# Mixture-of-experts inside a two-block layer: the experts' TensorE instructions kept in written order, and SwiGLU with one vector instruction less

## The chip, the cores and the metric

The kernel runs on one core of a Trainium2 chip. The metric is the device time of one execution in microseconds (us); the time before is given as the median of three runs.

## The reference

Two transformer blocks follow each other on 256 tokens of 1024 features, all in float32. The first has an RWKV and an attention mixer, then a mixture of 32 experts; the second has a stick-breaking attention, an attention over 256 memory tokens and a dense layer of 4096 hidden units. The change lies in the experts. Every token goes to 4 of them, and each does this (cut):

```python
gu = xb @ w_gate_up[e] + b_gate_up[e]
gate = jnp.minimum(gu[:, :D_FF], SWIGLU_LIMIT)                  # 7.0
up = jnp.clip(gu[:, D_FF:], -SWIGLU_LIMIT, SWIGLU_LIMIT)
act = (up + 1.0) * gate * jax.nn.sigmoid(SWIGLU_ALPHA * gate)   # 1.702
return act @ w_down[e] + b_down[e]
```

## The kernel before, in words

The first block up to the routing takes the first 277 us or so, the experts the time up to about 1260 us, the second block the rest. Each of the 32 experts has 64 slots for tokens (a branch for experts with more follows the stage and is there whether it is taken or not).

**Weights.** An expert's weights come in six transfers of 2 MB each, four for the gate and up matrices and two for the down matrix, through one queue of SyncE (`stream`, line 110, called by `issue`, line 1021). They go into nine slots of SBUF, shared out by `slot`; a transfer is issued when the chunk that had its slot before is used up. Ahead of expert 21 one slot is given up for the memory tokens' keys and values and one is lent to their weights. The last expert's last transfer comes in four pieces of 512 KB. Behind it the same queue fetches the first two weight chunks of the second block.

**An expert on the engines.** `gate_up` (line 1104) has TensorE multiply the inputs `xe` of 64 tokens with the weights, k by k, into two PSUM banks, `pg` (gate) and `pu` (up), after the biases (`bgu`, three bfloat16 parts) went in by a matmul of their own. Then SwiGLU: four instructions of VectorE and one sigmoid of ScalarE make `u`. `down` (line 1127) transposes `u` on TensorE (`at`), ScalarE copies the result, and TensorE multiplies it with the down weights (`py`); VectorE puts the product, times the gate of the modulation, into `y`.

**Two at a time.** `gather` (line 1066) fetches the inputs of two experts by a matmul with a one-hot matrix that VectorE builds (`s`; `ga`), and transposes the weighted one-hot (`sw`; `swt`). `combine` (line 1149) adds what two experts made to their tokens, by a matmul (`cb`) that VectorE adds to x. In the program they stand between an expert's `gate_up` and its `down`: the gather after every odd expert, the sum after every even one but the first:

```python
act = gate_up(e, ws[:4])
if e % 2 and e + 1 < ne:
    gather(e + 1)
if e % 2 == 0 and e:
    combine(e - 2)
down(e, act, ws[4:])
```

**What sets the order.** Each engine runs its instructions in one fixed order. A scheduler with a timeline of its own sets that order when the program is built; it may move an instruction past others that it doesn't depend on. The order on TensorE is therefore not that of the program text.

**After the experts.** The second block transposes x (`x3t`, copied to `xh` and `xl`), and multiplies it with weights that ScalarE and VectorE or GpSimd split in a high and a low part first (`w3h` and `w3l`, lines 117 and 118; matmuls `d`, lines 1274 to 1276). The buffers of the split parts lie where the experts' buffers were.

Of the kernel before, what the change touches and what calls it, by code (L numbers as in the profile page):

```python
# [10 lines left out]
F32 = mybir.dt.float32  # L11
# [4 lines left out]
OP = mybir.AluOpType  # L16
# [7 lines left out]
# plain PSUM banks before the experts; buffers of the RWKV and of the stick-breaking attention; how many experts  # L24
# before the last one the memory tokens come in
NP, B4, NZ, ME = 4, 5, 5, 12

# columns of the packed per-feature vectors
# [14 lines left out]
# columns of the constants (they depend on shapes alone)  # L43
# [47 lines left out]

class Kernel:
# [11 lines left out]
    # ---- weights stream: one order, one queue, a ring of slots  # L104
# [8 lines left out]
    def split(self, pool, src, n, name, eng):  # L113
        """src = hi + lo exactly, each in float32r"""
        hi = pool.tile([128, n], F32R, tag=name + "h", name=name + "h")
        lo = pool.tile([128, n], F32R, tag=name + "l", name=name + "l")
        self.nc.scalar.activation(hi, src, AF.Copy)  # L117
        eng.tensor_tensor(lo, src, hi.bitcast(F32), op=OP.subtract)  # L118
        return hi, lo
# [21 lines left out]
    def setup(self):  # L141
# [9 lines left out]
        # what is not needed past the experts  # L151
        self.xe = ExitStack()
        cp = self.pool("cpe", es=self.xe)
        # x after the attention, its scale per token, and the norm's gain and shift with the modulation, per feature
# [28 lines left out]
    def rsqrt(self, out, src, eps=None, scale=1.0, refine=None):  # L183
        """(src * scale + eps) ** -0.5; with a pool to take temporaries from, one Newton step more"""
# [25 lines left out]
    # ================================================================ first block, before the experts  # L210
    def expert_bias(self, pool):
        """the gate and up biases as three exact bfloat16 parts, on 3 x 32 partitions"""
# [4 lines left out]
        nc.sync.dma_start(t[0:32], A["b_gate_up"])  # L217
        for i in range(3):
# [5 lines left out]
    def phase1(self):  # L224
# [9 lines left out]
        # ---- modulation rows: silu(c) @ w_ada + b_ada; the i-th 512 columns add up on the partitions i mod 32  # L234
# [7 lines left out]
        # two slots of the stream that are at first lent to the RWKV and the MoBA  # L242
# [24 lines left out]
        def gate_rows():  # L267
            """rows 4, 5, 10 and 11, for the gates: partition by partition, the bias on one of them"""
# [14 lines left out]
        def gate_bc(q):  # L283
            """a row of a gate on every partition"""
# [4 lines left out]
        def ada_col(r, i0):  # L289
            """rows i0..i0+3 as columns [feature, (row, 128 features)]"""  # L290
# [6 lines left out]
        # ---- x over its root mean square, transposed  # L297
# [29 lines left out]
        # ---- h = rms(x) * g1 * (1 + scale1) + shift1, transposed, as hi + lo  # L327
# [19 lines left out]
        # ---- projections  # L347
# [10 lines left out]
        def dense_T(src, ncols, tiles, consume):  # L358
            """features on partitions; tiles: (first column, columns) of the chunk; two to a bank"""
# [13 lines left out]
        def dense_N(src, consume, then=lambda: None):  # L373
            """tokens on partitions, 512 columns"""
# [21 lines left out]
        def shift_mix(dst, ps, m, mi):  # L396
            """p + (shift(p) - p) * mu"""
# [45 lines left out]
        # ---- RWKV, element by element: decays inside chunks of 64 steps, scaled keys and receptances  # L443
# [9 lines left out]
        for g in ((0, 2), (2, 4)):  # L453
# [3 lines left out]
            # k * k_k over its norm per head  # L457
# [10 lines left out]
            # k * (1 + (a - 1) * k_a)  # L468
# [18 lines left out]
        # ---- RWKV, chunk by chunk: two chunks of 64 steps side by side, eight heads  # L487
# [10 lines left out]
        def pairs(lhs, rhs, tt, name):  # L498
            """per head, [step of lhs, step of rhs]; even heads, then odd ones"""
# [8 lines left out]
        def sub(s):  # L508
            """superchunk s: everything that needs neither the inverse nor the state"""
# [11 lines left out]
            # (I - L)^T of every 16 steps, kept as [row, head, column of the block]  # L521
# [4 lines left out]
        def invert(s, r):  # L526
            """(I - L)^T of every 16 steps: column r times row r of L^T goes to the columns after r"""
# [22 lines left out]
        # ---- MoBA projections (one block, so plain causal attention with ALiBi)  # L550
# [1033 lines left out]
```

## Time and profile before

| what | us |
|---|---|
| median of three runs | 1592.47 |
| the three runs | 1592.47, 1597.8, 1590.65 |
| span of the profiled execution | 1590.6 |
| TensorE busy | 1449.3 (91%) |
| VectorE busy | 591.2 (37%) |
| ScalarE busy | 395.1 (25%) |
| transfers, mean over the span | 318 GB/s |

The profiled execution's own time is that of its span, 1590.6 us; it equals the fastest of the three runs. Busy shares are means over stages with different limits. A matmul in float32 has two records in the trace. A busy TensorE isn't one at its peak, and the granted clock has a line of its own. PE is TensorE, DVE VectorE, ACT ScalarE, POOL GpSimd, SP SyncE. A wait is put down to the instruction that came last.

### The profile page before, as it was taken

To read this page: it belongs to the slowest core of one execution; us is meant where nothing else is said; L and a number is where in the kernel's file an instruction comes from. 1 tells how busy PE (TensorE), PEld (TensorE's weight loads), DVE (VectorE), ACT (ScalarE), POOL (GpSimd) and SP (SyncE) were. 2 spreads that over 40 slices of the span, in tenths; PEclk is the share of its full clock that TensorE was granted. 3 is DMA by queue.
4 is the path that set the end of the run, shared out by engine and by line. 5 is a ranking of instruction groups with operands and counts; after the bars stand their busy time and mean duration, and the time that the engine had idled before them with its cause. 6 is when DMAs were issued, how large, how long until landed. Compare 5 with 4: busy or idle time off the path is not lost. (4 is left out here: it accounts for less than half of the span.)

```text
span 1590.6 us, 19145 instructions
## 1 busy us (share of the span) xinstructions
PE 1449.3 (91%) x7818; PEld 813.4 (51%) x7818; DVE 591.2 (37%) x1177; ACT 395.1 (25%) x767; POOL 212.6 (13%) x190
## 2 busy tenths in 40 slices
PE   5999998999999989988998989999989899899996
PEld 2976876333333323323333334433333497699995
DVE  2576877232122222221222122222221345555455
ACT  4862344110000000000001011110010366455553
POOL 1243751000000000000000000000000233252221
PEclk9999999999999999999999999999999999989998
DMA  9734747899999999999999997999999451535540
GB/s 337 251 120 170 280 170 288 340 417 416 418 416 416 418 418 415 419 418 415 418 418 415 397 409 319 411 416 416 418 417 414 154 208 54 195 123 180 191 159 27
DMA packets 115061, 505.15 MB, mean 318 GB/s; under 512 B 5548, under 2 KB 6572, under 8 KB 82168
## 3 DMA queue, kind: packets, MB, share of 16 engines
q1 hardware_dynamic: 114792, 503.74, 79.9%
q8 instruction: 63, 1.03, 0.3%
q14 instruction: 30, 0.25, 0.0%
q0 software_dynamic: 176, 0.14, 0.0%
HBM read 502.81 MB, written 1.05 MB: 317 GB/s over the span
## 5 line engine op out<-in xcount | busy, mean ns | idle before, releaser
L1139 PE MATMUL py<-w,at 128*64 128x512 f32 x1024 | 265.0, 669 | 22.0 <-ACT at L1134 21.8
L1117 PE MATMUL pg<-w,xe 128*64 128x512 f32 x1024 | 267.7, 598 | 0.0
L1117 PE MATMUL pu<-w,xe 128*64 128x512 f32 x1024 | 264.9, 592 | 0.0
L1121 ACT ACTIVATE sg<-g 128x512 f32<-128x512 f32 (+1 forms) x33 | 20.2, 616 | 601.6 <-DVE g L1120 601.6
L1139 PEld LDWEIGHTS py<-w,at 128*64 128x64 f32 x1024 | 77.4, 153 | 175.7 <-issue 141.6
L1146 DVE TENSOR_TENSOR y<-py,gate 64x512 f32<-64x512 f32 x64 | 44.1, 688 | 304.4 <-PE py L1139 303.7
L1117 PEld LDWEIGHTS pu<-w,xe 128*64 128x64 f32 x1024 | 74.1, 137 | 146.7 <-issue 146.6
L117 ACT ACTIVATE w3h<-w 128x512 fp32r<-128x512 f32 x184 | 115.2, 631 | 109.1 <-PE d L1275 57.6
L1117 PEld LDWEIGHTS pg<-w,xe 128*64 128x64 f32 x1024 | 70.9, 137 | 135.0 <-issue 130.2
L118 DVE TENSOR_TENSOR w3l<-w,w3h 128x512 fp32r<-128x512 f32 x132 | 94.2, 719 | 115.7 <-ACT w3h L117 111.0
L1120 DVE TENSOR_SCALAR g<-pg 128x512 f32<-128x512 f32 (+1 forms) x33 | 22.2, 675 | 295.4 <-PE pg L1117 295.4
L118 POOL TENSOR_TENSOR w3l<-w,w3h 128x512 fp32r<-128x512 f32 x52 | 67.4, 1301 | 432.1 <-ACT w3h L117 420.9
L1274 PE MATMUL d<-xh,w3h 128*128 128x256 f32 x352 | 100.5, 288 | 0.9 <-ACT xh L1261 0.9
L1210 POOL TENSOR_TENSOR wml<-w,wml 128x512 fp32r<-128x512 f32 x4 | 5.2, 1293 | 718.5 <-ACT wml L1209 718.5
L1275 PE MATMUL d<-xl,w3h 128*128 128x256 f32 x352 | 100.8, 287 | 0.1
L1276 PE MATMUL d<-xh,w3l 128*128 128x256 f32 x352 | 100.2, 286 | 0.0
L1133 PE MATMUL at<-ca,u 128*128 128x128 f32 x128 | 23.5, 313 | 63.8 <-DVE u L1124 63.8
L1083 PEld LDWEIGHTS ga<-s,xm 128*128 128x128 f32 x512 | 62.3, 197 | 28.2 <-issue 26.5
L1083 PE MATMUL ga<-s,xm 128*128 128x128 f32 x512 | 69.8, 288 | 1.2 <-DVE s L1073 1.2
L1274 PEld LDWEIGHTS d<-xh,w3h 128*128 128x128 f32 x352 | 68.4, 196 | 1.6 <-ACT xh L1261 1.3
L1275 PEld LDWEIGHTS d<-xl,w3h 128*128 128x128 f32 x352 | 68.4, 194 | 0.9 <-DVE xl L1263 0.6
L1276 PEld LDWEIGHTS d<-xh,w3l 128*128 128x128 f32 x352 | 68.2, 194 | 0.0
(421 smaller groups left out, 2100.6 us busy)
## 6 DMA issues: line engine op xcount, KB each, us to landing
w<-w_gate_up SPq DMA_DIRECT2D x128, 2048.0 KB, 16.7
w<-w_down SPq DMA_DIRECT2D x71, 2048.0 KB, 17.6
w<-w_ada SPq DMA_DIRECT2D x12, 2048.0 KB, 9.2
w<-w_up SPq DMA_DIRECT2D x8, 2048.0 KB, 7.5
w<-w_in SPq DMA_DIRECT2D x6, 2048.0 KB, 11.4
w<-w_in_sb SPq DMA_DIRECT2D x5, 2048.0 KB, 10.3
w<-w_out SPq DMA_DIRECT2D x4, 2048.0 KB, 7.7
w<-w_mem_kv SPq DMA_DIRECT2D x1, 2048.0 KB, 12.0
```

Source lines behind the costliest of these rows:

```text
L117: self.nc.scalar.activation(hi, src, AF.Copy)
L118: eng.tensor_tensor(lo, src, hi.bitcast(F32), op=OP.subtract)
L1083: PE.matmul(ps[:, k * 128:(k + 1) * 128], xm[:, a, (kk + k) * 128:(kk + k + 1) * 128], s[:, a], start=a == 0, stop=a == 1, skip_group_chec ...
L1117: PE.matmul(p[64 * h:64 * h + 64, :], xe[:, k], w[:, k % 2, c:c + 512], start=False, stop=k == 7)
L1120: DVE.tensor_scalar(g[:, c], pg[:, c], 7.0, None, op0=OP.min)
L1121: ACT.activation(s[:, c], g[:, c], AF.Sigmoid, scale=1.702)
L1133: PE.transpose(ps[:, j * 128:(j + 1) * 128], act[:, j * 128:(j + 1) * 128], ident)
L1139: PE.matmul(py[64 * h:64 * h + 64, :], at[:, j, c], ws[c][:, j, h * 512:(h + 1) * 512], start=c == 0 and j == 0, stop=c == 1 and j == 3)
L1146: DVE.tensor_tensor(st[e & ~1][2][r, hs], py[64 * h:64 * h + 64], self.gate2[64 * h:64 * h + 64, hs], op=OP.mult)
L1274: PE.matmul(o, wh[:, ws], xh[:, k], start=k == 0 and i % 2 == 0, stop=False, skip_group_check=True)
L1275: PE.matmul(o, wh[:, ws], xl[:, k], start=False, stop=False, skip_group_check=True)
L1276: PE.matmul(o, wl[:, ws], xh[:, k], start=False, stop=k == 7, skip_group_check=True)
```

## The change

1. The experts' matmuls and transposes go through a small class `InOrder`, which ties each to the one before it by a dependency without a semaphore, so that the scheduler leaves them in the order of the program text. The matmuls of the down bias (`bias_down`) and those of the memory tokens are issued as before, outside this chain.
2. SwiGLU: the sigmoid reads the gate's bank directly and is clamped afterwards at sigmoid(1.702 x 7) (`SIG_MAX`), the clamp of the gate goes into the multiplication, and the 1.0 that is added to `up` is added once to its bias (so its clamp runs from -6 to 8). VectorE has three instructions instead of four for each expert, and the tile `g` is gone.
3. For the last point one VectorE instruction is added where the biases are prepared.

The comments and docstrings of the program are dropped as well. The diff, cut:

```diff
+SIG_MAX = 1.0 / (1.0 + math.exp(-1.702 * 7.0))
...
+class InOrder:
+    def __init__(self, tc, last=None):
+        self.tc, self.last = tc, last
+
+    def _keep(self, i):
+        if self.last is not None:
+            self.tc.add_manual_dep(i.ins, self.last.name,
+                                   mybir.DependencyInfo(mybir.DependencyClass.NoSync, mybir.DependencyReason.DATA),
+                                   reason="in order")
+        self.last = i.ins
+        return i
+
+    def matmul(self, *a, **k):
+        return self._keep(self.tc.nc.tensor.matmul(*a, **k))
+
+    def transpose(self, *a, **k):
+        return self._keep(self.tc.nc.tensor.transpose(*a, **k))
...
     def expert_bias(self, pool):
...
         nc.sync.dma_start(t[0:32], A["b_gate_up"])
+        DVE.tensor_scalar(t[0:32, 1024:2048], t[0:32, 1024:2048], 1.0, None, op0=OP.add)
...
     def experts(self):
         nc, A = self.nc, self.A
-        PE, ACT, DVE, POOL = nc.tensor, nc.scalar, nc.vector, nc.gpsimd
+        PE, ACT, DVE, POOL = InOrder(self.tc), nc.scalar, nc.vector, nc.gpsimd
...
-            g, u, s = (pool.tile([128, 512], F32, tag=n, name=n, bufs=1) for n in ("g", "u", "sg"))
+            u, s = (pool.tile([128, 512], F32, tag=n, name=n, bufs=1) for n in ("u", "sg"))
             for c in cuts(e):
-                DVE.tensor_scalar(g[:, c], pg[:, c], 7.0, None, op0=OP.min)
-                ACT.activation(s[:, c], g[:, c], AF.Sigmoid, scale=1.702)
-                DVE.tensor_scalar(u[:, c], pu[:, c], 7.0, -7.0, op0=OP.min, op1=OP.max)
-                DVE.scalar_tensor_tensor(u[:, c], u[:, c], 1.0, g[:, c], op0=OP.add, op1=OP.mult)
-                DVE.tensor_tensor(u[:, c], u[:, c], s[:, c], op=OP.mult)
+                ACT.activation(s[:, c], pg[:, c], AF.Sigmoid, scale=1.702)
+                DVE.tensor_scalar(u[:, c], pu[:, c], 8.0, -6.0, op0=OP.min, op1=OP.max)
+                DVE.scalar_tensor_tensor(u[:, c], pg[:, c], 7.0, u[:, c], op0=OP.min, op1=OP.mult)
+                DVE.scalar_tensor_tensor(u[:, c], s[:, c], SIG_MAX, u[:, c], op0=OP.min, op1=OP.mult)
```

**Order on TensorE, an odd expert in the middle of the stage.** Before, in a row: the gather `ga` for the next pair, in pieces between the down projection of the expert before and the odd expert's own gate and up matmuls, and further on the end of these.

```order
L1083 MATMUL ga<-s,xm 128x128 x3
L1139 MATMUL py<-w,at 64x512 x8
L1083 MATMUL ga<-s,xm 128x128 x4
L1117 MATMUL pg<-w,xe 64x512 x2
L1117 MATMUL pu<-w,xe 64x512 x2
L1117 MATMUL pg<-w,xe 64x512 x2
L1117 MATMUL pu<-w,xe 64x512 x2
L1083 MATMUL ga<-s,xm 128x128 x7
```

```order
L1117 MATMUL pg<-w,xe 64x512 x2
L1117 MATMUL pu<-w,xe 64x512 x2
L1133 MATMUL at<-ca,u 128x128 x4
L1139 MATMUL py<-w,at 64x512 x8
L1110 LDWEIGHTS selb
```

With the change, the same place (L109 and L112 are the lines of the class `InOrder`):

```order
L109 MATMUL pg<-w,xe 64x512 x2
L109 MATMUL pu<-w,xe 64x512 x2
L109 MATMUL ga<-s,xm 128x128 x16
L112 MATMUL swt<-ca,sw 128x128 x2
L112 MATMUL at<-ca,u 128x128 x4
L109 MATMUL py<-w,at 64x512 x16
```

The gather and the transposes of `sw` now stand whole between the last gate and up matmuls and the transposes `at`, which followed these directly before.

**Order on TensorE, the even expert behind it**, with the change; before, the sum `cb` stood between the gate and up matmuls too:

```order
L109 MATMUL pg<-w,xe 64x512 x2
L109 MATMUL pu<-w,xe 64x512 x2
L109 MATMUL cb<-y,swt 128x512 x4
L112 MATMUL at<-ca,u 128x128 x4
L109 MATMUL py<-w,at 64x512 x16
L109 LDWEIGHTS selb
```

The sum has the gather's place here; the next expert's biases (`selb`) come after the whole down projection.

**Order on VectorE, an odd expert**, before:

```order
L1120 TENSOR_SCALAR g<-pg 128x512
L1122 TENSOR_SCALAR u<-pu 128x512
L1123 SCALAR_TENSOR_TENSOR u<-u,g 128x512
L1089 TENSOR_SCALAR xe<-ga,sc_71,sh_72 128x128 x2
L1124 TENSOR_TENSOR u<-u,sg 128x512
L1089 TENSOR_SCALAR xe<-ga,sc_71,sh_72 128x128 x2
L1146 TENSOR_TENSOR y<-py,gate_74 64x512 x2
```

and with the change:

```order
L1146 TENSOR_SCALAR u<-pu 128x512
L1147 SCALAR_TENSOR_TENSOR u<-pg,u 128x512
L1148 SCALAR_TENSOR_TENSOR u<-sg,u 128x512
L1114 TENSOR_SCALAR xe<-ga,sc_71,sh_72 128x128 x2
L1098 TENSOR_SCALAR s<-ca,Rm,rs 128x64 x4
L1098 TENSOR_SCALAR sw<-ca,Rm,W 128x64 x4
L1114 TENSOR_SCALAR xe<-ga,sc_71,sh_72 128x128 x2
L1170 TENSOR_TENSOR y<-py,gate_74 64x512 x2
```

SwiGLU has one row less, and it is through before VectorE copies the gathered inputs out; the one-hot matrices `s` and `sw` of the pair after the next are built right behind.

## Rows read from the trace of the kernel before

**Rows 1.** The page: span, TensorE's busy time, and clock and DMA in 40 slices.
```profile
span 1590.6 us, 19145 instructions
...
PE 1449.3 (91%) x7818; PEld 813.4 (51%) x7818; DVE 591.2 (37%) x1177; ACT 395.1 (25%) x767; POOL 212.6 (13%) x190
...
PEclk9999999999999999999999999999999999989998
DMA  9734747899999999999999997999999451535540
```

**Rows 2.** Waits of TensorE, 300 to 1260 us: total, times, longest, in us.
```profile
PE at L1133 <- DVE u L1124: 63.8, 25, 2.9
PE py L1139 <- ACT at L1134: 21.8, 31, 1.2
```

**Rows 3.** Timeline of TensorE from 560 us: start, duration, in brackets the idle time before.
```profile
561.64 1.08 PE L1133 MATMUL at<-ca,u 128*128 128x128 f32 x4 [2.85 <-DVE u L1124]
563.41 6.03 PE L1139 MATMUL py<-w,at 128*64 128x512 f32 x16 [0.69 <-ACT at L1134]
...
593.23 0.63 PE L1133 MATMUL at<-ca,u 128*128 128x128 f32 x4 [2.40 <-DVE u L1124]
594.54 3.65 PE L1139 MATMUL py<-w,at 128*64 128x512 f32 x16 [0.69 <-ACT at L1134]
...
623.82 0.63 PE L1133 MATMUL at<-ca,u 128*128 128x128 f32 x4 [2.85 <-DVE u L1124]
```

**Rows 4.** Timeline of TensorE, 362 to 445 us, two of the first experts.
```profile
383.12 3.84 PE L1083 MATMUL ga<-s,xm 128*128 128x128 f32 x32
...
387.01 0.60 PE L1133 MATMUL at<-ca,u 128*128 128x128 f32 x4
388.30 7.09 PE L1139 MATMUL py<-w,at 128*64 128x512 f32 x32 [0.69 <-ACT at L1134]
...
409.48 3.70 PE L1155 MATMUL cb<-y,swt 128*128 128x512 f32 x8
413.02 0.60 PE L1133 MATMUL at<-ca,u 128*128 128x128 f32 x4
```

**Rows 5.** Timeline of VectorE in the same two experts.
```profile
385.13 0.69 DVE L1124 TENSOR_TENSOR u<-u,sg 128x512 f32<-128x512 f32 x1 [0.47 <-DVE u L1123]
...
411.53 0.68 DVE L1124 TENSOR_TENSOR u<-u,sg 128x512 f32<-128x512 f32 x1
```

**Rows 6.** Stretches: busy us (records) of each engine, clock, DMA share, GB/s.
```profile
320.00:840.00 520.00, 474.00 (x2179) 180.41 (x2176) 128.07 (x254) 39.27 (x81) 0.00 (x0) 0.96 1.02 417
840.00:960.00 120.00, 108.35 (x484) 40.79 (x486) 26.13 (x53) 9.09 (x19) 1.34 (x1) 0.93 1.00 404
960.00:1000.00 40.00, 36.45 (x194) 18.17 (x192) 9.20 (x16) 7.01 (x15) 2.56 (x2) 0.96 0.79 319
```

**Rows 7.** SyncE's waits, 300 to 900 us; DMA issues (count, KB, median us to landing).
```profile
SPq L110 <- PE pu L1117: 258.3, 66, 9.7
...
w<-w_gate_up SPq DMA_DIRECT2D x128, 2048.0 KB, 16.7
```

**Rows 8.** SyncE's issues at the end of the stage; issues there, as in rows 7.
```profile
1215.59 5.20 SPq L110 DMA_DIRECT2D w<-w_down  x5
...
w<-w_down SPq DMA_DIRECT2D x4, 512.0 KB, 11.8
```

**Rows 9.** Timeline of TensorE at the end of the stage.
```profile
1248.55 7.09 PE L1139 MATMUL py<-w,at 128*64 128x512 f32 x32
...
1261.56 1.94 PE L1248 MATMUL x3t<-ca,x 128*128 128x128 f32 x16 [1.44 <-DVEq L953]
1263.25 0.48 PE L1274 MATMUL d<-xh,w3h 128*128 128x256 f32 x2
```

**Rows 10.** Timeline of ScalarE there.
```profile
1255.68 4.27 ACT L117 ACTIVATE w3h<-w 128x512 fp32r<-128x512 f32 x8 [6.85 <-PE py L1139]
1262.35 2.07 ACT L1261 ACTIVATE xh<-x3t 128x512 fp32r<-128x512 f32 x4 [2.39 <-PE x3t L1248]
```

**Rows 11.** Timeline of VectorE at the start.
```profile
20.29 2.28 DVE L222 TENSOR_TENSOR bt<-bt,bgu 32x2048 f32<-32x2048 f32 x1 [1.63 <-ACT bgu L220]
```

More of the change, by code (lines that the diff above doesn't have):

```diff
@@ L1055, in bias_down @@
             for a in range(2):
-                PE.transpose(ps[0:32, a * 128:(a + 1) * 128], W[:, a], ident)
+                nc.tensor.transpose(ps[0:32, a * 128:(a + 1) * 128], W[:, a], ident)
             ACT.activation(wt, ps[0:32, 0:T], AF.Copy)
@@ L1062, in bias_down @@
                     ps = self.psum("bd")
-                    PE.matmul(ps, wt[:, a * 128:(a + 1) * 128], bd[:, hs], start=True, stop=True)
+                    nc.tensor.matmul(ps, wt[:, a * 128:(a + 1) * 128], bd[:, hs], start=True, stop=True)
                     DVE.tensor_tensor(x1[:, a, hs], x1[:, a, hs], ps, op=OP.add)
```

## The prediction

> **What bounds the kernel now.** I read the page first. TensorE is busy 91% of the span and the DMA share stands at its top digit from about 320 to 1240 us [rows 1], so two resources look like the bound of the expert stage, and the question is which of them would still be one if the other got faster.
>
> The waits of TensorE in that stage come next [rows 2]: 63.8 us in 25 places in front of the transposes, which wait for VectorE's last SwiGLU instruction, and 21.8 us in 31 places in front of the down projection. No wait for a weight transfer is in the list. One expert is seen in the order of time [rows 3]: transposes start at 561.64, 593.23 and 623.82, so an expert takes 31.6 and 30.6 us, with 2.4 to 2.9 us of standing still each time. After the longer one the granted clock was at the lower of its two levels (1.2 instead of 2.4 GHz) for a while: the first 16 records of the down projection took 6.03 us there against 3.65 us in the next expert.
>
> The same view holds a direct measurement of the order that the change asks for. In the first experts the scheduler left the written order alone [rows 4]: the gather (3.84 us) or the sum (3.70 us) stands right before the transposes, these have no wait, and transposes start at 387.01 and 413.02: 26.0 us for an expert. VectorE's last SwiGLU instruction is over at 385.13 + 0.69 = 385.82 and at 411.53 + 0.68 = 412.21 [rows 5], 1.2 and 0.8 us before the transposes need it, with the old SwiGLU at that.
>
> Last the transfers [rows 6]. From 320 to 840 us they ran at 417 GB/s and share 1.02, a stretch that holds both the 26.0 us experts and the 31 us ones: the rate did not move with TensorE's pace. An expert's six transfers of 2048 KB (2.097 MB) are 12.58 MB; at 417 GB/s that is 30.2 us. SyncE does wait for TensorE to free slots [rows 7], which looks as if TensorE set the pace, but from issue to landing a transfer takes 16.7 us at the median against 5.03 us of its own at 417 GB/s, so three are in flight while it waits. So TensorE with its waits (about 30.6 us) and the transfers (30.2 us) are nearly level, and TensorE without them (26.0 us) is well below. **The floor under this change is the transfers'.**
>
> **The change part by part.**
>
> Order. 25 waits of about 2.55 us go, because the gather or the sum now covers them. The clock spells behind them go too: 30.6 - 26.0 = 4.6 us for an expert, over 100 us of TensorE in all. Most of it is not time. By TensorE alone the 28 experts after 387.01 would be through at 387 + 28 x 26.0 = 1115 us; the transfers can't be. What is late next is the weight chunk. So the sum goes by the last landing and what follows it.
>
> (1) Last landing. SyncE issued the last four 512 KB pieces by 1220.8, they land 11.8 us after issue [rows 8], so about 1232.4. In 960 to 1000 us the stream ran at 319 GB/s, because TensorE was behind with the memory tokens and slots came late: (417 - 319) / 417 x 40 = 9.4 us lost. From 840 to 960 it ran at 404: another 3.7 us, though part of that may be the memory tokens' own transfers. A TensorE that comes to this place ahead gives the slots in time. Gain between 9.4 and 13.1; I take 11. Landing: 1221.4.
>
> (2) TensorE behind the last landing. Its last down projection ends at 1248.55 + 7.09 = 1255.6 [rows 9], 23.2 us after the landing, because TensorE is that far behind with chunks that lie ready. At 26.0 against 30.2 us it catches up 4.2 us with each expert, and is level long before the end. Then only the last piece's 4 of 32 records remain, 0.9 us. Gain 22.3.
>
> (3) Given back at the hand-over. The second block's first weights now land after the experts' end: one chunk of 5.0 us behind 1221.4, 1226.4. ScalarE splits it in eight instructions, 4.27 us, and these stand in its queue ahead of the copies of the transposed x [rows 10]; before, they began at 1255.68, when the down projection was over, and hid under the last sum. Now they end at 1230.7, the first copy starts then, and the block's first matmul 0.9 us later (1263.25 - 1262.35), at 1231.6. Without this it would follow the down projection by 1263.25 - 1255.6 = 7.6 us, at 1229.9. Cost 1.7. From there on the second block is TensorE's own work, as before.
>
> (4) Clock at the hand-over. TensorE now waits for chunks in the last experts and may enter the end at the lower level. One such spell cost 6.03 - 3.65 = 2.4 us [rows 3]. Between 0 and two of them; I take 2.
>
> (5) SwiGLU with one instruction less. 33 instructions of VectorE (0.69 us each) go, and the sigmoid reads the gate's bank directly. All of it lies under the gather or the sum, where there were already 0.8 to 1.2 us to spare [rows 5]: nothing, but for the first and the last expert, which have neither in front. Those waits shrink by at most the removed 0.69 us each; both are ahead of a chunk that is late anyway. I take 0. If the order did not hold, this cover would be gone and the shorter chain would be worth up to 0.69 us an expert.
>
> (6) The bias gets one added VectorE instruction at the start, over 32 partitions x 1024; the trace has 2.28 us for 2048 columns there [rows 11], so 1.1 us, in a queue whose next instructions feed the first norm. Between 0 (it starts when the bias has landed and VectorE is idle) and 1.1; I take 0.5.
>
> (7) The matmuls that the written order no longer brings forward (an expert's biases inside the down projection before it) cost the same at either place. SyncE's queue keeps its order but for one pair of chunks: nothing.
>
> Sum: -11 - 22.3 + 1.7 + 2 + 0.5 = -29.1 us. The profiled execution's span is 1590.6, equal to the fastest of the three runs shown (1590.65); the median, 1592.47, is 1.9 above. 1592.5 - 29.1 = 1563.4, so **1563 us**. The term to doubt is (2): 22 us rest on TensorE being level with the landings at the end. With the ends of (1), (3), (4) and (6) the case runs from about 1557 to 1571.
>
> One rule was weighed for the floor. The rows say 417 GB/s at share 1.02, whatever TensorE does. The Trainium skill (DMA: Bandwidth & Descriptors, section Bandwidth) gives 435 GB/s as the ceiling of the fabric and 425 measured for a large copy, which would leave the stream some speed to gain; by 435 the 901 us from 320 to 1221 would shrink by 37 us and the time would be near 1526, an estimate from that page. The trace disagrees so far, so the sum stays at 417.
>
> **Rivals.**
>
> The transfers have more to give (0.02). If 417 GB/s were the pace at which slots come free, TensorE's 26.0 us would become the stage's: about 132 us less, 1460. For it: SyncE's waits for TensorE [rows 7]. Against: at 26.0 us for an expert the stream would have had to run at 484 GB/s early on, and it stayed at 417.
>
> The wait moves instead of going (0.07). TensorE may now stand in front of the gather (for the one-hot or the evictions) or of the sum (for y), and keep some 4 us an expert. TensorE then stays about as far behind the landings, (2) brings nothing, and the memory tokens' gap stays: 1585 to 1594. The rows of the early experts [rows 4, 5] speak against it, since they have this order and no such wait.
>
> The clock (0.05, slower). A TensorE that waits for chunks stands still some 4 us in 30, in pieces, and each piece may leave it at 1.2 GHz for the next chunk. At that level 26.0 us of work are 52. It decides once an expert takes longer than today's 30.6 us, that is with more than 30% of the stage at the lower level: 26.0 / (1 - 0.3 / 2) = 30.6. With 40% it is 32.5 us, 28 experts x 1.9 = 53 us, 1645. For it: the spells behind standstills [rows 3] and page slices at 0.8 [rows 1]. Against: as soon as TensorE is the slower one it no longer waits, and in the experts that had only the 0.69 us stop [rows 4] the work ran at the full level. The Trainium skill (TensorE: Matmul & The Clock Gate, section on HAM oscillation) tells of a kernel that cooled down at every wait for a transfer and lost a good part of its time so; no stretch here shows that pattern. A mild form (one or two spells an expert, 0.04) only delays the catching up: 1573 to 1584.
>
> The order isn't changed (0.01): the engine's rows show that it is.
>
> **How the numbers follow.** Forecast 0.81, mild clock 0.04, moved wait 0.07, strong clock 0.05, more speed 0.02, no effect 0.01. A measurement of this kernel tells about 0.5%, 8 us, from no change. Faster by more: the forecast, most of the mild clock and the speed, 0.88; within: the moved wait and no effect, 0.07; slower: 0.05. The range runs from 1554, under the forecast's own end because the last landing rests on an average rate, to 1580, which takes in part of the mild clock.
>
> **What would show it.** Right: no wait of TensorE for VectorE's u in front of the transposes but in the first and last expert; waits for weight transfers of 1 us or more from the middle of the stage on; 416 to 418 GB/s through the memory tokens; last landing near 1221, and the second block's first matmul about 10 us behind it, near 1232. Wrong: transposes 30 us apart with waits on another cause, a rate under 410 or over 425, the lower clock level in a third of the stage, or a first matmul of the second block after 1250.

## The result, and the profile after

The change makes the kernel faster by a little over 1%: 1571.54 us, median of four runs (1567.94, 1568.55, 1574.53, 1576.28), against 1591.56 for the kernel before beside it; ratio 0.9862, 95% interval 0.9825 to 0.9899. The forecast was 1563, in a range of 1554 to 1580. The profiled execution is the one of 1568.55 us.

The page of the changed kernel, the lines that answer to [rows 1] and the GB/s in the same 40 slices:

```profile
span 1566.8 us, 19105 instructions
...
PE 1414.5 (90%) x7818; PEld 804.6 (51%) x7818; DVE 572.1 (37%) x1145; ACT 394.5 (25%) x767; POOL 212.9 (14%) x190
...
PEclk9998999899999999999999999999999999999998
DMA  9734747899999999999999999999999741525440
GB/s 335 262 118 148 265 166 285 339 419 415 418 418 416 416 418 417 416 417 419 416 416 418 416 413 416 417 418 416 418 417 417 285 162 54 215 108 202 175 162 28
```

From the ninth slice to the thirty-first the transfers have no dip any more (413 to 419 GB/s; the kernel before has 397, 409 and 319 in the 23rd to the 25th slice). The clock's digit is 9 there in both, too coarse to show its change. TensorE's busy time fell by 34.8 us with as many records as before (7818), 32.9 of them in the down projection's matmuls (`py`, 265.0 to 232.1 us), which used to stand behind the waits: that is the clock, whose mean over the span rose from 0.959 to 0.979.

Waits of TensorE from 280 to 1300 us, against [rows 2]:

```profile
PE pg L109 <- DMA w<-w_gate_up: 65.9, 59, 1.7
PE py L109 <- ACT at L1158: 20.6, 30, 0.7
PE at L112 <- DVE u L1148: 4.5, 3, 2.3
PE x3t L1272 <- PEq L978: 3.2, 1, 3.2
PE py L109 <- DMA w<-w_down: 2.5, 1, 2.5
```

The 25 waits for VectorE (63.8 us) are gone but for the first and the last expert (4.5 us), and 65.9 us of waiting for weight chunks stand in their place. All waits from 280 to 1300 us together are 98.5 us, against 89.6 before: there are not fewer, but what is waited for is another thing.

Stretches of the changed kernel, against [rows 6]:

```profile
320.00:840.00 520.00, 472.42 (x2266) 182.19 (x2264) 115.90 (x238) 40.11 (x82) 0.00 (x0) 1.00 1.02 417
840.00:960.00 120.00, 100.43 (x479) 39.95 (x476) 27.02 (x54) 10.08 (x21) 1.26 (x1) 0.99 1.02 415
960.00:1000.00 40.00, 38.63 (x227) 22.29 (x227) 10.46 (x25) 10.06 (x23) 3.85 (x3) 1.00 1.02 418
```

Up to 840 us the transfers ran at 417 GB/s before and run at 417 now. Between 840 and 1000, where they fell to 404 and 319 because TensorE was behind with the memory tokens, they now go on at 415 and 418. The gain comes from there and from the end of the stage. Timeline of TensorE at that end, against [rows 9]:

```profile
1214.30 1.08 PE L109 MATMUL pg<-w,xe 128*64 128x512 f32 x4 [1.30 <-DMA w<-w_gate_up]
...
1219.73 0.44 PE L112 MATMUL at<-ca,u 128*128 128x128 f32 x2 [1.77 <-DVE u L1148]
1220.60 0.44 PE L112 MATMUL at<-ca,u 128*128 128x128 f32 x2 [0.44 <-DVE u L1148]
1220.97 8.78 PE L109 MATMUL py<-w,at 128*64 128x512 f32 x32
1230.54 3.70 PE L109 MATMUL cb<-y,swt 128*128 128x512 f32 x8 [0.79 <-DVE y L1170]
1237.43 2.35 PE L1272 MATMUL x3t<-ca,x 128*128 128x128 f32 x16 [3.19 <-PEq L978]
1239.43 0.77 PE L1298 MATMUL d<-xh,w3h 128*128 128x256 f32 x2
```

The last weight piece is issued at 1205.24 with the change and at 1220.36 before. Its time from issue to landing, with the change (this piece alone) and before (the last four pieces; the last one has the 12.7):

```profile
DMA to landing us min/median/max: 19.3/19.3/19.3
```

```profile
DMA to landing us min/median/max: 10.1/11.8/12.7
```

So it lands at 1224.5 instead of 1233.0, and the last down projection ends at 1229.75, 5.25 us behind it (22.6 before). The second block's first matmul starts at 1239.43 instead of 1263.25: 23.8 us, which is the whole difference of the spans. What comes behind it takes 327.3 us in both.

### The profile page after: what moved, and what is told of

The parts are those of the page before. It is cut to its first block, busy times and chain, and to the rows that moved or that the text cites. A ratio compares the mean times of both kernels' runs of the same rounds, so it can differ in the third digit from the quotient of the medians.

```text
span 1566.8 us, 19105 instructions
## 1 busy us (share of the span) xinstructions
PE 1414.5 (90%) x7818; PEld 804.6 (51%) x7818; DVE 572.1 (37%) x1145; ACT 394.5 (25%) x767; POOL 212.9 (14%) x190
## 3 DMA queue, kind: packets, MB, share of 16 engines
q8 instruction: 63, 1.03, 0.3%
## 5 line engine op out<-in xcount | busy, mean ns | idle before, releaser
L109 PE MATMUL pg<-w,xe 128*64 128x512 f32 x1024 | 271.2, 600 | 65.9 <-DMA w<-w_gate_up 65.9
L109 PE MATMUL pu<-w,xe 128*64 128x512 f32 x1024 | 267.5, 592 | 0.0
L109 PE MATMUL py<-w,at 128*64 128x512 f32 x1024 | 232.1, 606 | 23.1 <-ACT at L1158 20.6
L1146 DVE TENSOR_SCALAR u<-pu 128x512 f32<-128x512 f32 (+1 forms) x33 | 22.2, 675 | 477.0 <-PE pu L109 477.0
L1145 ACT ACTIVATE sg<-pg 128x512 f32<-128x512 f32 (+1 forms) x33 | 19.3, 584 | 690.7 <-PE pg L109 689.0
L109 PEld LDWEIGHTS pg<-w,xe 128*64 128x64 f32 x1024 | 70.0, 137 | 217.5 <-issue 112.0
L109 PEld LDWEIGHTS py<-w,at 128*64 128x64 f32 x1024 | 72.3, 139 | 161.6 <-issue 133.3
L109 PEld LDWEIGHTS pu<-w,xe 128*64 128x64 f32 x1024 | 75.5, 137 | 145.8 <-issue 145.6
L109 PEld LDWEIGHTS ga<-s,xm 128*128 128x128 f32 x512 | 60.5, 197 | 13.5 <-issue 11.9
L109 PE MATMUL ga<-s,xm 128*128 128x128 f32 x512 | 63.6, 284 | 1.2 <-DVE s L1098 1.2
L109 PE MATMUL cb<-y,swt 128*128 128x512 f32 x128 | 59.2, 605 | 0.8 <-DVE y L1170 0.8
```

The lines of the kernel that those rows point to most:

```text
L109: return self._keep(self.tc.nc.tensor.matmul(*a, **k))
L1145: ACT.activation(s[:, c], pg[:, c], AF.Sigmoid, scale=1.702)
L1146: DVE.tensor_scalar(u[:, c], pu[:, c], 8.0, -6.0, op0=OP.min, op1=OP.max)
```

## The experiments

All times are medians; ratios are against the kernel before, run beside each on the same chip, where its own median lay between 1589.91 and 1596.03 us. A difference of a few us between medians from different chips therefore says nothing.

**Which of the two parts.** The order alone:

```diff
-        DVE.tensor_scalar(t[0:32, 1024:2048], t[0:32, 1024:2048], 1.0, None, op0=OP.add)
...
-                ACT.activation(s[:, c], pg[:, c], AF.Sigmoid, scale=1.702)
-                DVE.tensor_scalar(u[:, c], pu[:, c], 8.0, -6.0, op0=OP.min, op1=OP.max)
...
+                DVE.tensor_scalar(g[:, c], pg[:, c], 7.0, None, op0=OP.min)
+                ACT.activation(s[:, c], g[:, c], AF.Sigmoid, scale=1.702)
...
```

> The written order alone: SwiGLU as it was before (four VectorE instructions, the sigmoid behind the clamp) and no instruction for the biases. TensorE's instruction order is that of the changed kernel, line for line. If the transfers set the pace and SwiGLU lies under the gather or the sum, the time is that of the changed kernel, 1571 us, within 6 us; of the changed kernel's waits only the two of the first and the last expert get longer, by up to 0.7 us each. If the shorter SwiGLU carries part of the gain, 1580 us or more.

Measured 1568.76 us, ratio 0.9853 (0.9804 to 0.9901): the changed kernel's gain, whole. The waits for SwiGLU in the first and the last expert did not get longer either (4.3 us together against 4.5). SwiGLU alone is the complement:

```diff
-        PE, ACT, DVE, POOL = InOrder(self.tc), nc.scalar, nc.vector, nc.gpsimd
+        PE, ACT, DVE, POOL = nc.tensor, nc.scalar, nc.vector, nc.gpsimd
```

> The shorter SwiGLU and the bias instruction alone, without the fixed order. TensorE's instruction order is that of the kernel before, line for line, with 25 places where the transposes wait about 2.55 us for VectorE. Theory: each wait shrinks by one VectorE instruction at most (0.69 us), which takes TensorE's 30.6 us for an expert to 29.9 at best, just under the transfers' 30.2; the time then comes to 1580 to 1588 us, TensorE still behind the transfers at the end. Rival: the freed time is given back in clock spells or in the sum's place, and the time stays at 1589 to 1594. Other rival: SwiGLU is worth half or more of the gain, under 1580.

Measured 1597.69 us, ratio 1.0032 (1.0003 to 1.0060): no gain, if anything a loss, and outside what the theory and both rivals gave. TensorE's waits for u didn't shrink (63.8 us in 25 places before):

```profile
PE at L1157 <- DVE u L1148: 65.1, 26, 3.1
```

Why is seen in one expert of each. The kernel before, all engines from 588 us (start, duration, what was waited for):

```profile
589.79 1.03 PE L1117 MATMUL pu<-w,xe 128*64 128x512 f32 x4
590.01 0.69 DVE L1120 TENSOR_SCALAR g<-pg 128x512 f32<-128x512 f32 x1 [8.91 <-PE pg L1117]
590.80 0.63 ACT L1121 ACTIVATE sg<-g 128x512 f32<-128x512 f32 x1 [27.44 <-DVE g L1120]
590.87 0.69 DVE L1122 TENSOR_SCALAR u<-pu 128x512 f32<-128x512 f32 x1 [0.17 <-PE pu L1117]
591.60 0.69 DVE L1123 SCALAR_TENSOR_TENSOR u<-u,g 128x512 f32<-128x512 f32 x1
592.39 0.69 DVE L1124 TENSOR_TENSOR u<-u,sg 128x512 f32<-128x512 f32 x1
```

SwiGLU alone, the same:

```profile
599.32 1.03 PE L1142 MATMUL pu<-w,xe 128*64 128x512 f32 x4
...
600.39 0.69 DVE L1146 TENSOR_SCALAR u<-pu 128x512 f32<-128x512 f32 x1 [9.77 <-PE pu L1142]
601.19 0.69 DVE L1147 SCALAR_TENSOR_TENSOR u<-pg,u 128x512 f32<-128x512 f32 x1
601.91 0.69 DVE L1148 SCALAR_TENSOR_TENSOR u<-sg,u 128x512 f32<-128x512 f32 x1
602.75 0.63 PE L1157 MATMUL at<-ca,u 128*128 128x128 f32 x4 [2.40 <-DVE u L1148]
```

The removed clamp of the gate ran while TensorE was still at the last `pu` matmuls. Behind these, three instructions stand in a chain in both kernels, and the wait is 2.40 us in both ([rows 3] has it for this expert). The instruction that was removed was never on the path. Of the 10.7 us by which this profile's span is longer, 8.8 lie ahead of the first expert's transposes (309.11 against 300.27), where the granted clock was 0.55 between 180 and 200 us; the loss is therefore not shown to be SwiGLU's.

**Is the transfers' rate the floor.** Fewer bytes with the same work of TensorE, in the changed kernel and in the kernel before:

```diff
-                w = self.stream(d[:, 4 * j - 16:4 * j - 12], 4, 1024, pool, 4 if i == 6 * self.ne - 1 else 1)
+                n = 4 if j == 4 else 3
+                w = self.stream(d[:, 4 * j - 16:4 * j - 16 + n], n, 1024, pool, n if i == 6 * self.ne - 1 else 1)
...
-                        PE.matmul(py[64 * h:64 * h + 64, :], at[:, j, c], ws[c][:, j, h * 512:(h + 1) * 512],
+                        PE.matmul(py[64 * h:64 * h + 64, :], at[:, j, c], ws[c][:, min(j, 3 - c), h * 512:(h + 1) * 512],
```

> The changed kernel with the last 512 KB of every expert's second down chunk not loaded (the last quarter of that chunk's rows is replaced by the quarter before it, so the output differs); TensorE's work is the same, the bytes of an expert fall by 1/24. If the transfers are the floor of the stage, 1.26 us less for each of about 30 experts: 1530 to 1540 us, with the same GB/s. If TensorE or the hand-over of slots is the floor, 1565 to 1572.

> The kernel before with the same bytes left out. If TensorE with its waits (30.6 us for an expert) sets the pace there, the transfers being level at 30.2 and then 28.9, the time falls by 0 to 10 us only: 1582 to 1592, at a lower GB/s through the stage. If the transfers were already the floor before, it falls by as much as in the changed kernel, 30 to 40 us: 1553 to 1562.

Measured: 1529.2 us in the changed kernel, just under the expected 1530 to 1540, ratio 0.9607 (0.9554 to 0.9660), 2.6% or 41 us under the changed kernel's own; 1590.03 us in the kernel before, ratio 0.9978 (0.9950 to 1.0006), nothing. First stretch of each, the changed kernel's variant first:

```profile
320.00:840.00 520.00, 490.91 (x2380) 193.58 (x2378) 122.75 (x255) 43.31 (x89) 0.00 (x0) 0.99 1.02 417
```

```profile
320.00:840.00 520.00, 478.15 (x2180) 181.23 (x2178) 125.41 (x250) 38.60 (x80) 0.00 (x0) 0.95 0.99 401
```

The same bytes less are worth 41 us in the one and nothing in the other. With the change the stream stays at 417 GB/s and ends earlier; without it, it slows down to TensorE's pace. This pair shows the bound moving from TensorE to the transfers.

**How much room TensorE has.** Each gather's matmuls issued twice, and four times:

```diff
-                for k in range(4):
+                for k in [0, 1, 2, 3] * 2:
```

> The changed kernel with the matmuls of each gather issued twice: 3.84 us more of TensorE in every second expert, 1.9 us for an expert on the mean, 26.0 to 27.9 us against the transfers' 30.2. If the transfers are the floor, the time moves by 0 to 4 us: 1571 to 1576. If TensorE sets the pace, 16 gathers of 3.84 us, 61 us more: about 1630.

> The same with four times the matmuls of each gather: 11.5 us more in every second expert, 5.8 us on the mean, 26.0 to 31.8 us, over the transfers' 30.2. By the transfer floor at 30.2 us only what lies above it counts, 1.6 us for each of 28 experts, 45 us, and up to 20 us of TensorE's lag behind the last landing: 1616 to 1640 us. If TensorE set the pace of the changed kernel, 3 x 61 = 184 us: about 1755.

Measured: twice, 1571.41 us, ratio 0.9846 (0.9802 to 0.9890), the changed kernel's time. The gathers keep TensorE busy for 120.8 us instead of 63.6, 57 us more (61 were expected), and no time comes of it; the larger part came out of the waits for chunks. That for the gate and up chunks, in the changed kernel 65.9 us in 59 places, is now

```profile
PE pg L109 <- DMA w<-w_gate_up: 24.0, 21, 1.7
```

Four times, 1654.21 us, ratio 1.0369 (1.0324 to 1.0415): no such wait is left, and the stream runs at TensorE's pace again:

```profile
320.00:840.00 520.00, 508.55 (x2816) 252.34 (x2814) 105.13 (x214) 35.70 (x73) 0.00 (x0) 0.99 0.96 391
```

The sign and the place of the turn are as expected, the size is not: 83 us over the changed kernel instead of 45 to 65. Transposes are 37.1 and 26.0 us apart, 31.55 on the mean, as expected. The expectation left out the first gather, which stands ahead of the first expert (first transposes 11.8 us later), and the memory tokens' 17.5 us of TensorE (one distance of 54.6 instead of 37.1), which no longer hide; and it set all experts against 30.2 us, though the changed kernel's first eight distances are 27 us on the mean, with chunks that are there already.

**The hand-over.** Changes in two places were tried there, and the two together. The second block's second weight chunk behind the branch over the overflow:

```diff
-                    self.w3 = [self.stream(w_in[:, :, c * 512:(c + 1) * 512], 8, 512) for c in range(2)]
+                    self.w3 = [self.stream(w_in[:, :, c * 512:(c + 1) * 512], 8, 512) for c in range(1)]
```

> The changed kernel with the second of the two weight chunks of the second block issued behind the branch over the overflow instead of ahead of it. Theory: the branch takes TensorE 5.15 us instead of 3.33 because its instruction fetch stands behind the weight transfers still running; with one transfer less in the way it takes 3.3 to 4 us, the second block's first matmul comes 1 to 2 us earlier, and the time is 1569 to 1571, if the later chunk is not itself waited for (then up to 5 us more). Rival: the branch takes 5.1 us whatever runs beside it: no earlier first matmul.

The last two experts taken together:

```diff
+            if e >= self.ne - 2:
+                m = i - 6 * (self.ne - 2)
+                e, j = (self.ne - 2 + m // 4, m % 4) if m < 8 else (self.ne - 2 + (m - 8) // 2, 4 + m % 2)
...
+            if e == ne - 2:
+                w2 = [self.chunks.pop(6 * e + 6 + j) for j in range(6)]
+                act2 = gate_up(e + 1, w2[:4])
             down(e, act, ws[4:])
+            if e == ne - 2:
+                down(e + 1, act2, w2[4:])
```

> The changed kernel with the last two experts taken together: both experts' gate and up chunks are loaded ahead of both down chunks pairs, TensorE does both gate and up parts before the two down projections, and the last expert's SwiGLU is no longer cut in two. Theory: behind the last landing only the last piece's share of the last down projection remains, about 1 us, instead of 5.25 us: the last down projection ends 3 to 5 us earlier and the time is 1566 to 1569. Rival: the hand-over is bound by the second block's first weights (landing and ScalarE's split) and the branch, and 0 to 2 us come out.

Neither edit did what it says. The scheduler put the chunk of the first ahead of the branch again: all five engines have the changed kernel's order, so this is a repeat of it, 1567.51 us, ratio 0.9839 (0.9801 to 0.9876). In the second it moved an expert's down chunks ahead of the last expert's gate and up chunks again; TensorE waited 7.25 us for the first of these gate and up chunks, ran the first matmuls behind that wait at the lower clock level (1.97 us instead of 1.03 to 1.08), and the last down projection ended at 1234.16: 1571.03 us, ratio 0.9859 (0.9822 to 0.9896). Both were tried again with the order tied:

```diff
+    def behind(self, i):
+        return self.tc.issue_after(self.last_chunk) if i > 6 * (self.ne - 2) else ExitStack()
...
+                with self.behind(i):
+                    w = self.stream(g[:, 2 * j:2 * j + 2], 2, 2048, pool)
```

> The last pair again, this time with SyncE's queue tied to the order that was meant: the eight gate and up chunks of the last two experts, then their four down chunks, the last one in pieces. TensorE does both gate and up parts, then both down projections. Theory: behind the last landing (1224.5 us in the changed kernel) only about 1 us of the last down projection is left instead of 5.25, the second block's first matmul comes 3 to 4 us earlier, and the time is 1566 to 1569 us. Rival: TensorE's branch and the split of the second block's first weights, whose transfers end at 1229.8 and 1235.2 as before, hold the first matmul where it is: 0 to 1.5 us.

```diff
-                ACT.activation(xh[:, k:k + 2], v, AF.Copy)
+                i = ACT.activation(xh[:, k:k + 2], v, AF.Copy)
+                if gain is None and k == 0:
+                    t = self.ring.tile([128, 4096], F32, tag="w", name="w")
+                    self.w3.append(t.rearrange("p (k f) -> p k f", k=8))
+                    with tc.issue_after(i.ins):
+                        nc.scalar.dma_start(self.w3[1], A["w_in_sb_2"].rearrange("(k p) f -> p k f", p=128)[:, :, 512:1024])
```

> The changed kernel with the second weight chunk of the second block fetched through ScalarE's queue right after the first copy of the transposed x, so that it starts behind the branch over the overflow for certain; the first chunk has landed by then. Theory (the branch's instruction fetch stands behind running transfers): TensorE's branch takes 3.3 to 3.9 us, as in the kernels where no transfer ran beside it, instead of 4.4 to 5.2; the first matmul of the second block comes about 8 us after the last down projection instead of 9.7; the time falls by 1 to 2 us, unless the second chunk is waited for later. Rival (the branch is long for another reason, such as which instructions stand before it): 4.4 us or more again.

> Both edits together: last pair with ordered loads, and the second block's second chunk behind the branch. By the theories of the two: the last down projection ends about 1 us behind the last landing, the first matmul of the second block 8 us later, 1234 us, 5 us earlier than in the changed kernel; 1564 to 1567 us. If the hand-over is bound by the landing and split of the first weight chunk instead: 1568 to 1571.

Measured: last pair 1565.82 us, ratio 0.9822 (0.9791 to 0.9854); late chunk 1574.93, 0.9879 (0.9844 to 0.9914); both 1569.97, 0.9848 (0.9815 to 0.9880). With the pair's loads in order TensorE follows the landings, half a down projection at a time:

```profile
1207.17 3.65 PE L109 MATMUL py<-w,at 128*64 128x512 f32 x16 [0.97 <-DMA w<-w_down]
1212.17 3.65 PE L109 MATMUL py<-w,at 128*64 128x512 f32 x16 [1.35 <-DMA w<-w_down]
...
1217.37 7.09 PE L109 MATMUL py<-w,at 128*64 128x512 f32 x32 [0.96 <-DMA w<-w_down]
...
1233.15 3.60 PE L1287 MATMUL x3t<-ca,x 128*128 128x128 f32 x16 [4.22 <-PEq L978]
1236.40 0.58 PE L1313 MATMUL d<-xh,w3h 128*128 128x256 f32 x2
```

The down projection ends at 1224.46, 2.1 us behind the last landing (1222.4) instead of 5.25, nearly as meant; but from there to the first matmul it is 11.9 us instead of 9.7, so that of 3.2 us only about 1 is left. What takes it is TensorE's branch over the overflow, and the transposes behind it at the lower clock level (3.60 us instead of 2.35). The branch's row (duration in ns, three times the same; start) in the kernel before, the changed one, the last pair and the kernel with both edits, each followed by the first 2.5 us of it as a stretch, whose last two numbers are DMA share and GB/s:

```profile
L953 PEldq COMPARE_BRANCH  x1: 3327/3327/3327, 1257.8 to 1257.8; - x1
...
1257.80:1260.30 2.50, 2.32 (x6) 0.76 (x4) 1.99 (x4) 2.16 (x5) 2.50 (x3) 1.00 0.02 7
```

```profile
L978 PEldq COMPARE_BRANCH  x1: 5147/5147/5147, 1232.0 to 1232.0; - x1
...
1232.00:1234.50 2.50, 2.24 (x6) 0.69 (x4) 1.98 (x4) 2.36 (x5) 2.50 (x3) 1.00 0.48 180
```

```profile
L978 PEldq COMPARE_BRANCH  x1: 6267/6267/6267, 1226.6 to 1226.6; - x1
...
1226.60:1229.10 2.50, 2.33 (x6) 0.76 (x4) 1.99 (x4) 1.11 (x3) 0.40 (x1) 1.00 0.64 241
```

```profile
L978 PEldq COMPARE_BRANCH  x1: 3404/3404/3404, 1228.2 to 1228.2; - x1
...
1228.20:1230.70 2.50, 2.40 (x6) 0.76 (x4) 1.99 (x4) 1.21 (x3) 0.51 (x1) 1.00 0.10 34
```

The 14 profiles fall into two groups without an overlap. Where transfers ran beside the start of the branch at 180 to 241 GB/s (the changed kernel, its repeat, the order alone, the gather twice, the last pair) it took 4.37 to 6.27 us; in the nine others, at 7 to 58 GB/s, 3.33 to 3.83. The late chunk alone has 3.71 and both edits 3.40, as the theory said. It costs more than it brings, though, since the chunk is then waited for: both edits come to 1569.97 us, which is in the expectation's other range (1568 to 1571), but for this reason and not for the first chunk's. First wait of the two for the split weights, the late chunk and both edits:

```profile
1264.67 0.58 PE L1303 MATMUL d<-xh,w3h 128*128 128x256 f32 x1 [4.89 <-ACT w3h L140]
```

```profile
1250.66 0.39 PE L1318 MATMUL d<-xh,w3h 128*128 128x256 f32 x1 [3.10 <-ACT w3h L140]
```

The last run issues the chunk earlier, straight behind the branch, with the pair's loads in order:

```diff
+        one = pc.tile([128, 1], F32, tag="one", name="one")
+        i = ACT.activation(one, x[:, 0, 0:1], AF.Copy)
...
+        with tc.issue_after(i.ins):
+            nc.scalar.dma_start(self.w3[1], A["w_in_sb_2"].rearrange("(k p) f -> p k f", p=128)[:, :, 512:1024])
         xh, xl = transposed(x)
```

> The last pair with ordered loads again, and the second block's second chunk fetched through ScalarE's queue as the first thing behind the branch (behind a copy of one column of x) instead of behind the first copy of the transposed x. In the kernel with both edits TensorE's branch was down to 3.40 us, but the second chunk, issued at 1237.0 us, kept TensorE waiting 3.1 us at 1250.7. Theory: issued some 4 us earlier it is no longer waited for (under 1 us), the branch stays at 3.3 to 3.9 us, and the time is 1562 to 1567 us. Rival: issuing from ScalarE holds up its copies of the transposed x by as much, or the chunk still lands late: 1568 to 1572.

Measured 1564.66 us, ratio 0.9850 (0.9819 to 0.9880). The time lies in the theory's range and not in the rival's. The branch took 3.37 us and the wait for the split weights is gone, but what the rival named happened too: ScalarE stood in front of the issue from 1235.2 to 1237.7, the copies of the transposed x stood behind it, and TensorE waited 3.97 us for these instead. From the last down projection to the first matmul it is 11.8 us, as in the last pair (11.9):

```profile
1237.72 0.42 ACTq L1329 DMA_DIRECT2D w<-w_in_sb  x1
1238.24 2.07 ACT L1300 ACTIVATE xh<-x3t 128x512 fp32r<-128x512 f32 x4 [3.04 <-SPq L978]
```

So none of these kernels is shown to be faster than the changed one: the intervals of their ratios overlap with its own. The last pair's runs, 1563.29 to 1567.24, all lie below the changed kernel's four (1567.94 to 1576.28), but not below those of its repeat (1566.07 to 1576.73). The two lowest medians, 1564.66 and 1565.82, belong to kernels with the last pair in order; the third of that kind has 1569.97.

## Why the prediction was right, and where it was off

**The bound: right.** "The floor under this change is the transfers'" is shown by the pair with fewer bytes (41 us against nothing) and by the gather issued twice (57 us of TensorE for nothing). The order freed about 94 us of TensorE (59.3 of waits for SwiGLU and 34.8 of busy time; the text had over 100). Of these, 23.8 came out as time and 68.4 stand as waits for chunks.

**The order: right.** With the gather or the sum in front, the transposes wait only in the first and the last expert. From the fourth to the ninth, experts are 26.0 to 26.4 us apart. From the tenth on, level with the stream, it is 29.8 and 30.4 in turn, except around the memory tokens (up to 43.9, and 26.0 to 26.4 for three experts behind them, until TensorE is level again).

**(1) Last landing, 1221.4 forecast: 1224.5.** The forecast started from 1232.4 before, with the median of four pieces from issue to landing; the last one took longer and landed at 1233.0. From the first transposes the last landing is 922.7 us away (1224.5 - 301.81), against 932.7 before: a gain of 10.0, between the two bounds (11 were taken). So the stream was slow in the memory tokens' stretch because slots came late, as said: it now runs at 418 there, and at 415 instead of 404 ahead of it, together worth about 12.7 us by the text's own reckoning. Some of that is used up again: 384.5 MB are moved from the first transposes to the last landing instead of 383.7, about 2 us, probably because the second block's first chunks are now issued (1209.57 and 1211.44) ahead of that landing. The first transposes are 1.5 us later (301.81 instead of 300.27), which is not shown to be the change's doing. The 922.7 us are a property of the stage: in the order alone, the repeat, the late chunk, both edits and the last run it is 922.6 to 922.9, though these start between 299.28 and 310.70.

**(2) TensorE behind the last landing, 0.9 us forecast: 5.25.** The gain is 17.4 us (22.6 - 5.25) instead of 22.3. This term was the one that failed, by size: "then only the last piece's 4 of 32 records remain". TensorE was level, as said, but the last expert's own chain was overlooked. Its last gate and up chunk lands at 1214.3; behind that come 3.7 us of matmuls, SwiGLU with waits of 1.77 and 0.44, two transposes, and the whole down projection, while the stream needs 10.2 us for the two down chunks. The chain's length, not the last piece, sets the end. The run with the last pair in order took 3.2 us of it away (5.25 to 2.1), which shows it.

**(3) Given back at the hand-over, 1.7 us forecast.** The mechanism named was there but did not decide: ScalarE split the first chunk from 1230.09 to 1234.36, later than forecast (1226.4 to 1230.7), yet the x it had to copy came later still, at 1238.22. What decided was TensorE's branch, 5.15 us instead of 3.33, beside which the second block's chunks now run; the fourteen profiles above bear that out. From the end of the down projection to the first matmul it took 9.7 us instead of 7.6: 2.1. That this is close to the 1.7 is luck, since the reason is another.

**(4) Clock at the hand-over, 2 us forecast.** One spell in the last down projection (8.78 instead of 7.09 us, counted in the 5.25) and one at the first `d` (0.77 instead of 0.48): about 2. The reason is again not the one given: these spells stand behind waits for SwiGLU (1.77 us) and for the branch (3.19 us), not behind waits for chunks.

**(5) SwiGLU, 0: right,** and more so than the text had it: the "up to 0.69 us an expert" without the cover are 0, since the removed instruction ran under TensorE's last matmuls.

**(6) Bias instruction, 0.5 us.** It took 0.68 us, and the first projections start at 37.45 against 37.60: nothing on the path. **(7)** Nothing seen.

**The sum.** 23.8 us were gained where 29.1 were forecast, 5.3 less: 1.0 by (1), 1.0 by the later start (1.5 against the 0.5 of (6)), 4.9 by (2) (4.35 for the last expert's chain and 0.6 because the landing before was put too early), and 1.6 the other way, since (3) and (4), set at 3.7, left 2.1 behind the down projection. The second block took 327.3 us as before. One reading beside it was wrong: here 1.75 us lie around the span (1568.55 against 1566.8), so the profiled execution of the kernel before was rather that of 1592.47 than the one of 1590.65. The section on the time before calls the span and the fastest run equal; that they agree in figures is chance. The sum was made from 1592.5 and doesn't change; the median of after lies 3 us over its profiled execution. Two smaller sums don't come out: the ends given for (1), (4) and (6) make 1559 to 1568 and the text gives none for (3), so that 1557 to 1571 can't be followed; and the chances by direction add up to 0.87 faster and 0.08 within, not 0.88 and 0.07.

**The signs.** The waits moved as named, the rate through the memory tokens is the 416 to 418 named (418), and no sign of being wrong came up. Two of the places were off: the last landing at 1224.5 instead of 1221, and the first matmul of the second block at 1239.43, 14.9 us behind it, instead of 1232 and 10.

**The rivals.** More speed of the transfers: no slice of the stage stands over 419 GB/s, even with TensorE ahead. The Trainium skill (DMA: Bandwidth & Descriptors, section Bandwidth) gives 435 GB/s as the ceiling and 425 measured for a copy of 16 MB; no slice of any run here is over 420. Moved wait: false; the 1.2 us in front of one gather and the 0.8 in front of one sum are in the kernel before too. Strong clock: false. Standing still for chunks came in pieces of at most 1.7 us, 59 times, and left the granted clock at 0.99 to 1.00, the upper of the two levels. One wait was longer:

```profile
916.88 5.35 PE L109 MATMUL py<-w,at 128*64 128x512 f32 x16 [2.54 <-DMA w<-w_down]
```

Behind it the clock was at the lower level for a while (0.50 from 918 to 921 us), and those 16 records took 5.35 us instead of 3.65. Behind the one wait of 7.25 us, in the first run of the last pair, it was 0.55 for 6 us (1198.8 to 1204.8), next to the lower one. The Trainium skill (TensorE: Matmul & The Clock Gate, section on HAM oscillation) describes a kernel that cools down at every wait for a transfer; in this stage the traces show that behind waits at these two places only; in the last run a wait of 2.51 us at the same place was not followed by the lower level.

## What to carry to other kernels

A wait on the busiest engine is worth what the next resource leaves of it: work out both paces for one unit of work, here 26.0 and 30.2 us for an expert, and cost the change by the slower. Taking bytes away, and adding work to the engine, each by a known amount, tells in two runs which of them binds. Behind the last landing count the whole chain of the last unit, not the last piece; and look at what runs beside a branch or another hand-over once the stage ahead of it gets shorter.

## What the hardware showed unexpectedly

TensorE's branch takes 3.33 to 3.83 us when hardly a transfer runs beside its start (7 to 58 GB/s), and 4.37 to 6.27 at 180 to 241 GB/s. In the trace a packet of 16 KB with instructions came 0.93 us after the branch began in the kernel before and 2.57 us after it in the changed one. All 14 profiles agree on this: the packet comes 0.92 to 1.01 us after the beginning in the nine short branches and 1.80 to 3.58 in the five long ones, and the branch ends 2.4 to 2.9 us behind the packet's start in all of them. So the late packet accounts for the longer branch; that it is late because it queues behind the weights is likely, but not shown. Behind the branch SyncE goes on late. Its rows on the branch's line in the last run (ns; first and last start):

```profile
L978 SPq EVENT_SEMAPHORE  x8: 17/17/17, 1237.7 to 1238.4; - x8
L978 SPq COMPARE_BRANCH  x1: 53/53/53, 1232.5 to 1232.5; - x1
```

5.2 us lie between the branch and the semaphores behind it, and the transfer issued from ScalarE started within 0.3 us of the first of them in all three kernels that had one. What SyncE does in those 5 us wasn't tried.
